# Two of the four weight sums of a seven-product block formed by the loading DMA instead of by VectorE

## The chip, the cores and the metric

The kernel runs on one core of a Trainium2 chip. The metric is device time in microseconds (us) of one launch, from the first to the last instruction of the core. The engines of the core run as separate instruction streams and meet only at semaphores: TensorE (PE, matmuls; PEld, its weight loads), VectorE (DVE), ScalarE (ACT), GpSimd (POOL) and SyncE (SP). Plain loads and stores are issued by SP; GpSimd can issue transfers too, from a queue of its own.

## The reference

The reference is one inference step of a two-layer backbone over 640 tokens (128 context tokens and 512 latent ones) of width 1024. Each layer has an attention mixer followed by a SwiGLU feed-forward part (FFN), and the FFN is where the change lies:

```python
def swiglu(h, w_in, w_out):
    gate, up = jnp.split(h @ w_in, 2, axis=-1)
    return (jax.nn.silu(gate) * up) @ w_out
...
hp = modulate(rms_norm(xp, norm_ffn[l]), sh2_p, sc2_p)
hs = modulate(rms_norm(xs, norm_ffn[l]), sh2_s, sc2_s)
xp = xp + g2_p * swiglu(hp, w_ffn_in[l], w_ffn_out[l])
xs = xs + g2_s * swiglu(hs, w_ffn_in[l], w_ffn_out[l])
```

Everything is float32. `w_ffn_in` is 1024 x 5632 per layer (2816 gate columns and 2816 up columns), `w_ffn_out` is 2816 x 1024.

## The kernel before

**How a matmul is done.** Activations lie transposed, 128 features on the partitions and 640 tokens in the free dimension, in two halves of 320 tokens. Each float32 operand is split into a high part in the fast matmul format (fp32r) and the remainder, and each product is three matmuls (high times high and the two mixed ones). The split of a weight tile is one ScalarE copy (the high part) and one VectorE subtraction (the low part); the helper that does both is `split` (L1361, its two instructions L1367 and L1368).

**The seven-product blocks.** A hidden block `fb` is 128 gate columns and 128 up columns; there are 22 of them per layer. For most of them the products of gate and up weights with the two halves of tokens are not computed as eight quarter products but as seven, by a Strassen-like scheme that needs sums of quarters of the weights and sums of quarters of the activations. With the up weights `u` split into a first half `ua` and a second half `ub`, and the gate weights `g` into `ga` and `gb` (each 128 x 512 in the tile), the function `seven` (L1166) makes four weight sets: wX from `u` as loaded, wW from `gb`, wY from the pair s13 = (`ga` + `gb`, `ua` + `ga`), and wZ from the pair s24 = (`ua` + `ga` + `gb`, that plus `ub`). So four additions of 128 x 512, all on VectorE: L1176 and L1177 for s13, L1180 and L1181 for s24. s13 and s24 are tiles of one tag, "ws", which has two buffers, so that the tile of the next block's s13 is the one that this block's s24 (or s13) has just left.

**Which blocks.** Layer 0 makes blocks 4 to 21 in this way (18), layer 1 blocks 3 to 21 (19); the loop is L1480 to L1509. The output projection of layer 1 uses the same `seven` for 12 more blocks (class `Block`, L1216), four for each of three passes over pairs of hidden blocks. Of these, eight are 1024 columns wide and four 768. That makes 49 uses of `seven`.

**One block of the loop on each engine.** On TensorE a block is seven products of 12 matmuls, in the order p1 (wX), p5 (wY), E of the block before (wW), N (wZ), 21 (wX), 22 (wZ), C (wY). ScalarE and VectorE empty the PSUM banks after each: `p1`, `p5`, `u1` are ScalarE copies, the two additions into `up` and the addition `g2` are VectorE's (L1503, L1505, L1507), the gate function is ScalarE's and its product with `up` is VectorE's (`sg`, L1476). In layer 0 the finished hidden block is split into `hd` (L1427, L1428) and stored in DRAM (`sp`, L1433); in layer 1 seven operands of each pair of blocks are made from it (`op`, L1394, L1395) and stored likewise, to be loaded again in the output projection (`or`, L1278). In layer 0 VectorE also does the modulation sums of a later stage between the blocks (`junk`, L1627, on weights `wm` loaded through the same SP queue).

**What sets the order.** The instructions are emitted in program order and a scheduler places them on the engines; on each engine they then run strictly in the placed order. A tile's buffer is taken again when the last reader of the tile before has finished, which is a semaphore wait of the next writer. If that writer is a DMA, the queue that issues it (SP's or GpSimd's) stands until then, and everything behind it in that queue with it. Weight tiles are split about one block ahead of TensorE.

Of the kernel before, what the change touches and what calls it, by code (L numbers as in the profile page):

```python
# [11 lines left out]
F32 = mybir.dt.float32  # L12
F32R = mybir.dt.float32r
AF = mybir.ActivationFunctionType
ALU = mybir.AluOpType
# [3 lines left out]
P = 128  # L19
# [32 lines left out]
def body(ctx, tc, xT, vecs, crow, wm0, wm0g1, wm0g, wm1, wA, wNV, wNA, wMK, wMV, wOA, wGQ, wGK, wGV, wOC,  # L52
         wFI, wFO, wFO1, cckvT, ckrT, cnkT, cnv, cgkT, cgv, rpbp, tabM, tabK, tabG, maskN,
         yT, o_ckvT, o_krT, o_nkT, o_nv, o_gkT, o_gv):
    nc = tc.nc
    V, S, G = nc.vector, nc.scalar, nc.gpsimd
# [32 lines left out]
    def bank(name, kind="m"):  # L89
        if kind == "m":  # L90
            return psp.tile([P, 512], F32, tag="m", bufs=4, name=name)
        return ypool["pool"].tile([P, 512], F32, tag=kind, bufs=ypool["tags"][kind], name=name)
# [10 lines left out]
    def tmp(name):  # L103
        return tp.tile([P, T], F32, tag="t", bufs=3, name=name)

    def f(ap):
        return ap.bitcast(F32)
# [55 lines left out]
    def load(src, n, name):  # L163
        raw = rawp.tile([P, 1024], F32, tag="raw", name=name)
        nc.sync.dma_start(raw[:, :n], src)
        return raw[:, :n]
# [177 lines left out]
    def mod0(j, bk, load_):  # L344

        box = []

        def part(half):
            def run():
                if half == 0:  # L350
                    box.append(bk())
                psm, rs = box[0], load_(j, half)

                for g in range(4):
                    for b in range(2):
                        o = 512 * (g % 2) + 256 * b
                        rows = slice(64 * b + 32 * (g % 2), 64 * b + 32 * (g % 2) + 32)
                        PE.matmul(psm[rows, :256], scol[:, 4 * half + g, :], rs[g // 2][:, o:o + 256], start=half == 0 and g < 2,
                                  stop=half == 1 and g > 1, tile_position=(0, rows.start))
                if half == 1:  # L360
                    box.append(tp.tile([P, HT], F32, tag="u", bufs=7, name=f"modsb{j}"))
                    S.activation(box[1][:, :256], psm[:, :256], AF.Copy)
            return run

        def end():
            psm, sb = box
            for i in range(2):
                PE.matmul(psm[:, 4 * i:4 * i + 4], sb[:, i * P:(i + 1) * P], sel, start=True, stop=True)
            for i, t in enumerate(MOD0[j]):
                V.tensor_tensor(mods[0][:, t:t + 2, :], psm[:, 0:8].rearrange("p (a i b) -> p a i b", a=2, b=2)[:, :, i, :],  # L370
                                bc2(bmod(0, t, 2)), ALU.add)
        return [part(0), part(1), end]
# [139 lines left out]
    with tc.tile_pool(name="start", bufs=1) as big:  # L512
# [14 lines left out]
        m = [mod0(j, lambda j=j: bank(f"mod{j}", "m"), lambda j, half: [raws[j, half][:, q, :] for q in range(2)]) for j in range(4)]  # L527
# [91 lines left out]
    for kk in range(4):  # L619
# [3 lines left out]
        for j in range(2):  # L623
            k = 2 * kk + j
            a, b = wh[:, 512 * j:512 * (j + 1)], wl[:, 512 * j:512 * (j + 1)]
            for i in range(5):
                c0, c1 = P * i, P * i + P
# [256 lines left out]
    for h in range(8):  # L884
        p, r = divmod(h, 2)
# [116 lines left out]
    for h in range(8):  # L1002
        p, r = divmod(h, 2)
# [159 lines left out]
                w.append(unit(wFI[l, 0, i], 1024, f"wgu{l}_{i}", "vg"[i], pool=fp))  # L1163
        return ph, fk, dr, hd, fs, fp, w, (su, scratch), pre

    def seven(ru, rg, name, fp, split):  # L1166

        n = ru.shape[-1]
        m = n // 2
        wX = split(ru, f"wX{name}")  # L1170
        t = fp.tile([P, 2, 512], F32R, tag="w4", bufs=2, name=f"wW{name}")
        wW = t[:, 0, :m], t[:, 1, :m]
        S.activation(wW[0], rg[:, m:], AF.Copy)
        V.tensor_tensor(wW[1], rg[:, m:], f(wW[0]), ALU.subtract)
        s13 = fp.tile([P, 1024], F32, tag="ws", bufs=2, name=f"s13{name}")[:, :n]
        V.tensor_tensor(s13[:, :m], rg[:, :m], rg[:, m:], ALU.add)  # L1176
        V.tensor_tensor(s13[:, m:], ru[:, :m], rg[:, :m], ALU.add)  # L1177
        wY = split(s13, f"wY{name}")
        s24 = fp.tile([P, 1024], F32, tag="ws", bufs=2, name=f"s24{name}")[:, :n]
        V.tensor_tensor(s24[:, :m], s13[:, m:], rg[:, m:], ALU.add)  # L1180
        V.tensor_tensor(s24[:, m:], s24[:, :m], ru[:, m:], ALU.add)  # L1181
        wZ = split(s24, f"wZ{name}")
        return wX, wW, wY, wZ

    def ffn_out_seven(x, nxt, opened, ops, spilt, split, close, last):
# [6 lines left out]
        def raw(n, c0, m, name):  # L1192
            raws[0] += 1
            t = (rawp.tile([P, 1024], F32, tag="raw", name=name) if raws[0] % 4 else
                 fp.tile([P, 1024], F32, tag="wr", bufs=1, name=name))[:, :m]
            nc.sync.dma_start(t, wFO1[n, :, c0:c0 + m])
            return t
# [18 lines left out]
        class Block:  # L1216


            def __init__(self, i, n, c0):
                self.pairs, self.n, self.name = PASSES[i], n, f"o{i}_{n}"  # L1220
                self.end = i == len(PASSES) - 1
                self.m = m = P * len(self.pairs)
                ru, rg = raw(n, c0, 2 * m, f"ru{self.name}"), raw(n + 4, c0, 2 * m, f"rg{self.name}")
                self.wX, self.wW, self.wY, self.wZ = seven(ru, rg, self.name, fp, split)
                self.held = {}

            def go(self, ps, wt, j, what, first):
# [63 lines left out]
        prev, c0 = None, 0  # L1291
# [41 lines left out]
        for b in ends:  # L1333
# [5 lines left out]
            t = weighed[b.n + 4] = tp.tile([P, HT], F32, tag="u", bufs=7, name=f"xw{b.n}")  # L1339
# [17 lines left out]
    def ffn(l, x, pend, hm, nxt, side, opened):  # L1357
# [123 lines left out]
        for fb in range(few, FB):  # L1481

            ru = load(wFI[l, fb, 1], 1024, f"wu{l}_{fb}r")
            if fb == few or l and fb % 2:
                rg = load(wFI[l, fb, 0], 1024, f"wg{l}_{fb}r")
            else:
                rg = fp.tile([P, 1024], F32, tag="wr", bufs=2 - l, name=f"wg{l}_{fb}r")
                nc.sync.dma_start(rg, wFI[l, fb, 0])
            wX, wW, wY, wZ = seven(ru, rg, f"{l}_{fb}", fp, split)

            g, b5, b2 = bank(f"fg{l}_{fb}"), bank(f"fd{l}_{fb}"), bank(f"fu{l}_{fb}", "y")
            up, sg = tmp(f"up{l}_{fb}"), tmp(f"sg{l}_{fb}")
            p1, p5, u1, g2 = [utile(f"{n}{l}_{fb}") for n in ("p1", "p5", "u1", "g2")]
            product(g, wX, 0, 11, True)
            S.activation(p1, g[:, :HT], AF.Copy)
            product(b5, wY, 0, "D", True)
            S.activation(p5, b5[:, :HT], AF.Copy)  # L1497
            if job:
                close(job)
            product(g, wZ, 0, "N", False)  # L1500
            S.activation(u1, g[:, :HT], AF.Copy)
            product(b2, wX, 512, 21, True)
            V.tensor_tensor(up[:, 0:HT], b2[:, :HT], p1, ALU.add)  # L1503
            product(b5, wZ, 512, 22, False)
            V.tensor_tensor(up[:, HT:T], b5[:, :HT], u1, ALU.add)  # L1505
            product(g, wY, 512, "C", False)
            V.tensor_tensor(g2, g[:, :HT], p5, ALU.add)  # L1507
            S.activation(sg[:, HT:T], g2, AF.Silu, scale=-1.0)
            job = fb, g, wW, up, sg  # L1509
# [48 lines left out]
        pss, ws = {}, {}  # L1558
# [127 lines left out]
    ws = [unit(wGK[v], 1024, f"wgk{v}") for v in range(2)]  # L1686
# [198 lines left out]
    _, before = mod_side([(1, wm1[G2:], G2)], None)  # L1885
# [172 lines left out]
```

## Time and profile before

| What | Value |
|---|---|
| median of 3 runs | 1500.65 us (1499.55 to 1503.75) |
| the profiled execution | 1503.23 us, of which the span of the instructions is 1501.2 us |
| granted TensorE clock | 0.995 of full speed (mean) |
| TensorE busy | 1448.7 us, 96% of the span |
| VectorE busy | 1233.7 us, 82% |
| ScalarE busy | 786.2 us, 52% |
| GpSimd busy | 176.3 us, 12% |
| SP's DMA queue | 225.43 MB, 45.0% of the 16 DMA engines' time |

The FFN loop of layer 0 lies at about 433 to 660 us, that of layer 1 at about 1118 to 1330 us, and the output projection of layer 1 from there to about 1470 us. In a row of a timeline the first number is the start in us, the second the duration, then come engine, line, operation, the tile written and the tiles read, and in brackets how long the engine had been idle and what released it. Names of tiles in the trace are cut: `s` is s13 or s24 of the loop, `s13o` and `s24o` those of the output projection, `wg_12r` and `wu_12r` the loaded gate and up weights of block 12. "SPq" and "POOLq" are DMA issues by SP and GpSimd. In the list of DMA issues the last number is the median time from issue to landing.

### The profile page before, as it was taken

How to read it: one execution, taken by the hardware profiler on the slowest of the kernel's cores; microseconds unless marked ns; L12 is line 12 of the kernel's file. 1: busy time of each engine (PE TensorE's matmuls, PEld its weight loads, DVE VectorE, ACT ScalarE, POOL GpSimd, SP SyncE). 2: the span in 40 equal slices, each digit the busy share in tenths (PEclk: the TensorE clock that was granted, in tenths of full speed). 3: DMA queues.
4: the chain of work that ended last, by engine and by line, in shares of the span. 5: the costliest groups of instructions: out<-in, count | busy, mean ns of one | idle time of the engine just before them, and what ended most of it. 6: DMA issues, size and time to landing. Idle time of an engine off the chain costs nothing. (4 is left out here: it accounts for less than half of the span.)

```text
span 1501.2 us, 25833 instructions
## 1 busy us (share of the span) xinstructions
PE 1448.7 (96%) x9766; PEld 1392.8 (93%) x9766; DVE 1233.7 (82%) x2375; ACT 786.2 (52%) x1539; POOL 176.3 (12%) x272
## 2 busy tenths in 40 slices
PE   5999989899999999999999999999999999999997
PEld 4989978889899999999999999989899999999996
DVE  5877778877788888955898887887899989889976
ACT  5446677763635555532122656673565555655443
POOL 0046636420000000000000122220100000000000
PEclk9999999999999999999999999999999999999999
DMA  9653341015055555549775311115245555548561
GB/s 375 202 152 121 114 145 43 15 64 204 29 207 164 170 171 168 162 169 341 231 229 169 103 33 36 37 41 185 68 157 169 193 170 191 175 154 297 181 263 71
DMA packets 79636, 231.48 MB, mean 154 GB/s; under 512 B 8856, under 2 KB 13240, under 8 KB 79128
## 3 DMA queue, kind: packets, MB, share of 16 engines
q1 hardware_dynamic: 77152, 225.43, 45.0%
q10 hardware_dynamic: 1944, 3.48, 0.7%
q8 instruction: 76, 1.25, 0.3%
q0 software_dynamic: 416, 0.93, 0.2%
q14 instruction: 48, 0.39, 0.1%
HBM read 193.15 MB, written 36.66 MB: 153 GB/s over the span
## 5 line engine op out<-in xcount | busy, mean ns | idle before, releaser
L1627 DVE SCALAR_TENSOR_TENSOR junk<-wm,cb 128x1024 bf16<-128x1024 f32 x88 | 107.2, 1218 | 3.4 <-DMA wm<-in_wm 2.8
L64 PE MATMUL gq<-h10h,wgq 128*128 128x320 f32 x256 | 65.8, 316 | 0.0
L261 POOL TENSOR_SCALAR h10h<-h10t,gs,mods 128x320 fp32r<-128x320 f32 x4 | 3.1, 787 | 437.7 <-DVE h10t L255 435.4
L1367 ACT ACTIVATE wY<-s 128x1024 fp32r<-128x1024 f32 x37 | 39.2, 1060 | 27.7 <-PE fg L64 24.0
L1893 POOL TENSOR_TENSOR xr<-xw,fn1rs 128x320 f32<-128x320 f32 x2 | 1.7, 860 | 416.9 <-ACT fn1rs L229 416.9
L1367 ACT ACTIVATE wZ<-s 128x1024 fp32r<-128x1024 f32 x37 | 39.1, 1057 | 18.6 <-PE fd L64 16.3
L1368 DVE TENSOR_TENSOR wZ<-s,wZ 128x1024 fp32r<-128x1024 f32 x37 | 45.2, 1222 | 2.9 <-ACT wZ L1367 0.2
L1476 DVE TENSOR_TENSOR sg<-up,sg 128x640 f32<-128x640 f32 x37 | 30.4, 822 | 20.8 <-ACT sg L1475 20.3
L64 PEld LDWEIGHTS gq<-h10h,wgq 128*128 128x128 f32 x256 | 44.9, 189 | 0.6
L1368 DVE TENSOR_TENSOR wY<-s,wY 128x1024 fp32r<-128x1024 f32 x37 | 45.1, 1218 | 0.3
L1475 ACT ACTIVATE sg<-fg 128x320 f32<-128x320 f32 x37 | 16.2, 438 | 48.5 <-PE fg L64 48.5
L64 PE MATMUL fg<-h01q,wgu 128*128 128x320 f32 x192 | 40.3, 316 | 0.9 <-ACT h01q L298 0.5
L1497 ACT ACTIVATE p<-fd 128x320 f32<-128x320 f32 x37 | 16.2, 438 | 46.7 <-PE fd L64 46.7
L1830 ACT ACTIVATE gp<-gs,gb,rq 128x640 f32<-128x640 f32 (+1 forms) x40 | 31.8, 795 | 15.3 <-DVE gb L1829 13.6
L64 PE MATMUL gq<-h10l,wgq 128*128 128x320 f32 x128 | 39.5, 308 | 0.0
L64 PE MATMUL fg<-h11q,wX 128*128 128x320 f32 x228 | 36.7, 309 | 0.0
L64 PE MATMUL fu<-h11q,wX 128*128 128x320 f32 x228 | 36.6, 309 | 0.0
L64 PE MATMUL fd<-h11q,wZ 128*128 128x320 f32 x228 | 36.6, 309 | 0.0
L64 PE MATMUL fg<-h11E,wW 128*128 128x320 f32 x228 | 36.5, 309 | 0.0
L64 PE MATMUL fg<-h11N,wZ 128*128 128x320 f32 x228 | 36.5, 309 | 0.0
L64 PE MATMUL fd<-h11D,wY 128*128 128x320 f32 x228 | 36.4, 308 | 0.0
L64 PE MATMUL fg<-h11C,wY 128*128 128x320 f32 x228 | 36.4, 308 | 0.0
(3399 smaller groups left out, 5323.0 us busy)
## 6 DMA issues: line engine op xcount, KB each, us to landing
wm<-in_wm SPq DMA_DIRECT2D x48, 512.0 KB, 4.2
mraw<-in_wm SPq DMA_DIRECT2D x8, 1024.0 KB, 13.1
mraw<-in_wm SPq DMA_DIRECT2D x16, 512.0 KB, 4.1
wmv<-in_wm0g SPq DMA_DIRECT2D x8, 512.0 KB, 3.9
wm<-in_wm0g SPq DMA_DIRECT2D x8, 512.0 KB, 5.3
ruo<-in_wFO SPq DMA_DIRECT2D x8, 512.0 KB, 4.0
rgo<-in_wFO SPq DMA_DIRECT2D x8, 512.0 KB, 6.0
x<-in_xT SPq DMA_DIRECT2D x8, 320.0 KB, 5.2
```

The source lines that it names most:

```text
L64: cls.last = nc.tensor.matmul(*a, **k)
L261: G.tensor_scalar(h[:, c0:c1], t, self.gsl[:, k, 0:1], self.ml[:, self.sh + k, 0:1], ALU.mult, ALU.add)
L1367: S.activation(h, src, AF.Copy)
L1368: V.tensor_tensor(w_, src, f(h), ALU.subtract)
L1475: last = S.activation(sg[:, 0:HT], g[:, :HT], AF.Silu, scale=-1.0)
L1476: V.tensor_tensor(sg, up, sg, ALU.mult)
L1497: S.activation(p5, b5[:, :HT], AF.Copy)
L1627: V.scalar_tensor_tensor(junk, raw, 1.0, cb[:, c, :], ALU.mult, ALU.mult, accum_out=mods[l][:, j0 + i, c:c + 1])
L1830: S.activation(dst, src, AF.Exp, bias=nb, scale=rq[:, j:j + 1], accum_out=ll[:, j:j + 1])
L1893: G.tensor_tensor(x[k][:, c0:c1], root[1][k], nrm.rs[:, c0:c1], ALU.mult)
```

## The change

A new function `first_sums` makes s13. SP loads `gb` into its first half and `ua` into its second half, plainly; then GpSimd issues two transfers that read `ga` from DRAM and add it into the one half and into the other. The two additions on VectorE (L1176, L1177) are gone. Since `ga` is no longer needed by itself, the gate load of a block shrinks to its second half, 128 x 512 (256 KB) instead of 128 x 1024 (512 KB). The up load stays. The s24 additions stay on VectorE and read s13 as before. Per full-width block the DMA engines thus bring 512 + 256 + 4 x 256 = 1792 KB where it was 1024 KB.

```diff
+    def first_sums(name, fp, m, gb, ua, ga):
+
+        t = fp.tile([P, 1024], F32, tag="ws", bufs=2, name=f"s13{name}")[:, :2 * m]
+        nc.sync.dma_start(t[:, :m], gb)
+        nc.sync.dma_start(t[:, m:], ua)
+        for j in range(2):
+            G.dma_start(t[:, j * m:j * m + m], ga, accum_op=ALU.add)
+        return t
+
-    def seven(ru, rg, name, fp, split):
+    def seven(ru, gb, s13, name, fp, split):
 
         n = ru.shape[-1]
         m = n // 2
         wX = split(ru, f"wX{name}")
         t = fp.tile([P, 2, 512], F32R, tag="w4", bufs=2, name=f"wW{name}")
         wW = t[:, 0, :m], t[:, 1, :m]
-        S.activation(wW[0], rg[:, m:], AF.Copy)
-        V.tensor_tensor(wW[1], rg[:, m:], f(wW[0]), ALU.subtract)
-        s13 = fp.tile([P, 1024], F32, tag="ws", bufs=2, name=f"s13{name}")[:, :n]
-        V.tensor_tensor(s13[:, :m], rg[:, :m], rg[:, m:], ALU.add)
-        V.tensor_tensor(s13[:, m:], ru[:, :m], rg[:, :m], ALU.add)
+        S.activation(wW[0], gb, AF.Copy)
+        V.tensor_tensor(wW[1], gb, f(wW[0]), ALU.subtract)
         wY = split(s13, f"wY{name}")
         s24 = fp.tile([P, 1024], F32, tag="ws", bufs=2, name=f"s24{name}")[:, :n]
-        V.tensor_tensor(s24[:, :m], s13[:, m:], rg[:, m:], ALU.add)
+        V.tensor_tensor(s24[:, :m], s13[:, m:], gb, ALU.add)
         V.tensor_tensor(s24[:, m:], s24[:, :m], ru[:, m:], ALU.add)
         wZ = split(s24, f"wZ{name}")
         return wX, wW, wY, wZ
...
-                ru, rg = raw(n, c0, 2 * m, f"ru{self.name}"), raw(n + 4, c0, 2 * m, f"rg{self.name}")
-                self.wX, self.wW, self.wY, self.wZ = seven(ru, rg, self.name, fp, split)
+                ru, gb = raw(n, c0, 2 * m, f"ru{self.name}"), raw(n + 4, c0 + m, m, f"rg{self.name}")
+                s13 = first_sums(self.name, fp, m, wFO1[n + 4, :, c0 + m:c0 + 2 * m], wFO1[n, :, c0:c0 + m], wFO1[n + 4, :, c0:c0 + m])
+                self.wX, self.wW, self.wY, self.wZ = seven(ru, gb, s13, self.name, fp, split)
...
             if fb == few or l and fb % 2:
-                rg = load(wFI[l, fb, 0], 1024, f"wg{l}_{fb}r")
+                gb = load(wFI[l, fb, 0, :, 512:], 512, f"wg{l}_{fb}r")
             else:
-                rg = fp.tile([P, 1024], F32, tag="wr", bufs=2 - l, name=f"wg{l}_{fb}r")
-                nc.sync.dma_start(rg, wFI[l, fb, 0])
-            wX, wW, wY, wZ = seven(ru, rg, f"{l}_{fb}", fp, split)
+                gb = fp.tile([P, 1024], F32, tag="wr", bufs=2 - l, name=f"wg{l}_{fb}r")[:, :512]
+                nc.sync.dma_start(gb, wFI[l, fb, 0, :, 512:])
+            s13 = first_sums(f"{l}_{fb}", fp, 512, wFI[l, fb, 0, :, 512:], wFI[l, fb, 1, :, :512], wFI[l, fb, 0, :, :512])
+            wX, wW, wY, wZ = seven(ru, gb, s13, f"{l}_{fb}", fp, split)
```

The change moves instructions on three queues. The names `s_12_6548` and `s_12_6554` below are s13 and s24 of block 12 before, `s_12_6558` and `s_12_6572` the same two after; lines L1368, L1503, L1505, L1507, L1476, L1428 before are L1375, L1511, L1513, L1515, L1483, L1435 after.

VectorE before, layer 0, from the low part of wZ of block 11 to that of block 12:

```order
L1368 TENSOR_TENSOR wZ_11_6420<-s_11_6417,wZ_11_6420 128x1024 [waits Activation_49]
L1507 TENSOR_TENSOR g_9_6165<-fg_9_6157,p_9_6163 128x320 [waits PE_49]
L1176 TENSOR_TENSOR s_12_6548<-wg_12r 128x512 [waits DMAHW3_49,DVE_49]
L1368 TENSOR_TENSOR wY_11_6414<-s_11_6411,wY_11_6414 128x1024 [waits Activation_49]
L1177 TENSOR_TENSOR s_12_6548<-wu_12r,wg_12r 128x512 [waits DMAHW4_49]
L1180 TENSOR_TENSOR s_12_6554<-s_12_6548,wg_12r 128x512 [waits DVE_49]
L1181 TENSOR_TENSOR s_12_6554<-s_12_6554,wu_12r 128x512 [waits DVE_49]
L1476 TENSOR_TENSOR sg_9_6161<-up_9_6160,sg_9_6161 128x640 [waits Activation_49]
L1174 TENSOR_TENSOR wW_11_6408<-wg_11r,wW_11_6408 128x512 [waits PE_49,Activation_49]
L1428 TENSOR_TENSOR hd_0l<-sg_9_6161,hd_0h 128x640 [waits DMAHW2_49,Activation_49]
L1503 TENSOR_TENSOR up_10_6296<-fu_10_6295,p_10_6298 128x320 [waits PE_49]
L1368 TENSOR_TENSOR wX_12_6542<-wu_12r,wX_12_6542 128x1024 [waits Activation_49]
```

VectorE after, the same place, from there to wZ of block 12:

```order
L1375 TENSOR_TENSOR wZ_11_6436<-s_11_6433,wZ_11_6436 128x1024 [waits Activation_49]
L1515 TENSOR_TENSOR g_9_6177<-fg_9_6169,p_9_6175 128x320 [waits PE_49]
L1375 TENSOR_TENSOR wY_11_6430<-s_11_6419,wY_11_6430 128x1024 [waits DMASW6_49,Activation_49]
L1483 TENSOR_TENSOR sg_9_6173<-up_9_6172,sg_9_6173 128x640 [waits DVE_49,Activation_49]
L1183 TENSOR_TENSOR wW_11_6427<-wg_11r,wW_11_6427 128x512 [waits PE_49,Activation_49]
L1186 TENSOR_TENSOR s_12_6572<-s_12_6558,wg_12r 128x512 [waits DMAHW2_49,DMASW1_49,DVE_49]
L1435 TENSOR_TENSOR hd_0l<-sg_9_6173,hd_0h 128x640 [waits Activation_49]
L1187 TENSOR_TENSOR s_12_6572<-s_12_6572,wu_12r 128x512 [waits DVE_49]
L1511 TENSOR_TENSOR up_10_6310<-fu_10_6309,p_10_6312 128x320 [waits PE_49]
L1375 TENSOR_TENSOR wX_12_6563<-wu_12r,wX_12_6563 128x1024 [waits Activation_49]
L1513 TENSOR_TENSOR up_10_6310<-fd_10_6308,u_10_6314 128x320 [waits PE_49]
L1375 TENSOR_TENSOR wZ_12_6575<-s_12_6572,wZ_12_6575 128x1024 [waits Activation_49]
```

The two additions of s13 are gone, the first addition of s24 has moved behind `sg` and wW of the block before, and it now waits for one of GpSimd's transfers (DMASW).

SP before, layer 0, around the loads of blocks 12 to 14:

```order
L1433 DMA sp_8h<-hd_2h 128x640 [waits DMAHW2_49,Activation_49]
L1488 DMA wg_12r<-in_wFI 128x1024 [waits DVE_49]
L1433 DMA sp_8l<-hd_2l 128x640 [waits DMAHW4_49,DVE_49]
L165 DMA wu_14r<-in_wFI 128x1024 [waits DMAHW5_49,DVE_49]
L1488 DMA wg_13r<-in_wFI 128x1024 [waits DMAHW6_49,DVE_49]
```

SP after, the same place:

```order
L1440 DMA sp_8h<-hd_2h 128x640 [waits DMAHW3_49,Activation_49]
L1440 DMA sp_8l<-hd_2l 128x640 [waits DMAHW4_49,DVE_49]
L165 DMA wu_14r<-in_wFI 128x1024 [waits DMAHW5_49,DVE_49]
L1169 DMA s_12_6558<-in_wFI 128x512 [waits DMASW5_49,DMASW4_49,DVE_49]
L1170 DMA s_12_6558<-in_wFI 128x512 [waits DMAHW7_49]
L1495 DMA wg_13r<-in_wFI 128x512 [waits DMAHW0_49,DVE_49]
```

The two plain loads of s13 stand behind the up load of block 14 and ahead of the gate load of block 13. The VectorE event that the first of them waits for is the low part of wZ of block 11, the last reader of the buffer that s13 of block 12 takes.

GpSimd after, the beginning of layer 0's loop (before, the rows L1172 were not there, and the others stood in this order):

```order
L384 TENSOR_SCALAR mp_3_4103<-mp_3_4103,mr_3r 128x640 [waits DVE_49,PE_49]
L384 TENSOR_SCALAR mpp3p<-mpp3p,mpp3r1r 128x128 [waits DVE_49]
L1172 DMA s_4_5497<-in_wFI 128x512 [waits DMAHW1_49,DMAHW0_49,DMAHW4_49,DMASW0_49,DVE_49]
L1172 DMA s_4_5497<-in_wFI 128x512 [waits DMAHW1_49,DMASW1_49]
L174 TENSOR_TENSOR wgu_1_4736<-wgu_1r,wgu_1_4736 128x1024 [waits DMAHW5_49,PE_49,Activation_49]
L301 TENSOR_SCALAR h01q_4769<-h0132a 128x320 [waits PE_49,Activation_49]
L301 TENSOR_SCALAR h01q_4771<-h0132a 128x320 [waits PE_49,Activation_49]
L301 TENSOR_SCALAR h01q_4773<-h0132a 128x320 [waits PE_49,Activation_49]
L301 TENSOR_SCALAR h01q_4775<-h0132d_4762 128x320 [waits PE_49,Activation_49]
L1172 DMA s_5_5609<-in_wFI 128x512 [waits DMAHW6_49,DMASW2_49,DMAHW7_49,DVE_49,Pool_49]
L1172 DMA s_5_5609<-in_wFI 128x512 [waits DMAHW0_49,DMASW3_49]
```

GpSimd's queue now holds two transfers for each block, each waiting for the plain load of its half; the pair of the first block stands ahead of a weight split (L174) and of four operand sums (L301) that belong to the blocks before the loop.

## The prediction

> **What bounds the kernel now.** I read the page's busy shares first, then the windows over the stages that use the seven-product blocks (stretch, length, busy time of PE, PEld, DVE, ACT and POOL, granted clock, DMA share, GB/s), then the timeline of one block.
>
> ```profile
> PE 1448.7 (96%) x9766; PEld 1392.8 (93%) x9766; DVE 1233.7 (82%) x2375; ACT 786.2 (52%) x1539; POOL 176.3 (12%) x272
> ...
> 460.00:640.00 180.00, 180.00 (x1230) 180.00 (x1230) 161.18 (x233) 94.56 (x147) 0.00 (x0) 1.00 0.52 165
> 1120.00:1300.00 180.00, 180.00 (x1230) 180.00 (x1230) 164.27 (x260) 105.76 (x184) 0.00 (x0) 1.00 0.54 177
> 1300.00:1350.00 50.00, 50.00 (x343) 50.00 (x343) 43.53 (x72) 27.93 (x51) 0.00 (x0) 1.00 0.47 155
> 1350.00:1400.00 50.00, 50.00 (x343) 49.98 (x343) 46.97 (x87) 26.30 (x43) 0.00 (x0) 1.00 0.88 306
> 1400.00:1450.00 50.00, 50.00 (x343) 50.00 (x342) 41.63 (x70) 20.78 (x29) 0.00 (x0) 1.00 0.68 240
> 1450.00:1501.00 51.00, 41.16 (x273) 39.86 (x271) 36.55 (x76) 19.58 (x39) 1.68 (x2) 0.94 0.19 69
> ```
>
> In both FFN loops TensorE is busy in all of the time shown, and the output projection is the same until 1450. VectorE is at 90% there and GpSimd does nothing. So in these stages work taken from VectorE is worth nothing by itself, and the only question is whether something new makes TensorE wait. Idle TensorE is left in the tail (51.0 - 41.2 = 9.8 us).
>
> ```profile
> 523.14 1.92 PE L64 MATMUL fg<-h01q,wX 128*128 128x320 f32 x12
> ...
> 535.45 1.93 PE L64 MATMUL fg<-h01q,wX 128*128 128x320 f32 x12
> ...
> 538.97 1.92 PE L64 MATMUL fg<-h01E,wW 128*128 128x320 f32 x12
> ```
>
> Product p1 comes back after 12.31 us: that is a block on TensorE.
>
> **What is removed.** The chain of one block on VectorE, with the SP issue and the ScalarE copy that matter:
>
> ```profile
> 520.91 1.22 DVE L1368 TENSOR_TENSOR wX<-wu_11r,wX 128x1024 fp32r<-128x1024 f32 x1
> 522.17 0.33 SPq L165 DMA_DIRECT2D wu_14r<-in_wFI  x1
> 522.68 1.23 DVE L1368 TENSOR_TENSOR wZ<-s,wZ 128x1024 fp32r<-128x1024 f32 x1
> 526.25 0.69 DVE L1176 TENSOR_TENSOR s<-wg_12r 128x512 f32<-128x512 f32 x1 [1.95 <-DMA wg_12r<-in_wFI]
> 528.00 0.68 DVE L1177 TENSOR_TENSOR s<-wu_12r,wg_12r 128x512 f32<-128x512 f32 x1
> 528.72 0.69 DVE L1180 TENSOR_TENSOR s<-s,wg_12r 128x512 f32<-128x512 f32 x1
> 529.44 0.69 DVE L1181 TENSOR_TENSOR s<-s,wu_12r 128x512 f32<-128x512 f32 x1
> 530.05 0.82 DVE L1476 TENSOR_TENSOR sg<-up,sg 128x640 f32<-128x640 f32 x1
> 531.68 0.83 DVE L1428 TENSOR_TENSOR hd_0l<-sg,hd_0h 128x640 fp32r<-128x640 f32 x1 [0.20 <-ACT hd_0h L1427]
> 532.42 0.48 DVE L1503 TENSOR_TENSOR up<-fu,p 128x320 f32<-128x320 f32 x1
> 533.22 1.23 DVE L1368 TENSOR_TENSOR wX<-wu_12r,wX 128x1024 fp32r<-128x1024 f32 x1 [0.32 <-ACT wX L1367]
> 534.37 0.48 DVE L1505 TENSOR_TENSOR up<-fd,u 128x320 f32<-128x320 f32 x1
> 534.98 1.23 DVE L1368 TENSOR_TENSOR wZ<-s,wZ 128x1024 fp32r<-128x1024 f32 x1
> 535.65 1.06 ACT L1367 ACTIVATE wY<-s 128x1024 fp32r<-128x1024 f32 x1 [0.70 <-PE fg L64]
> 536.13 0.48 DVE L1507 TENSOR_TENSOR g<-fg,p 128x320 f32<-128x320 f32 x1
> ```
>
> The two additions are 0.69 + 0.68 us of VectorE per block, at most 49 x 1.37 = 67 us in all. All of it lies beside a full TensorE except in the tail; I cost it at nothing. The shorter gate load is one 256 KB transfer less per block, also hidden.
>
> **What is added, and where it stands.** After the change s13 of block 12 is written by transfers, into the buffer that the low part of wZ of block 11 has left (522.68 + 1.23 = 523.91). In the order after, SP's first plain load waits for exactly that event; the two GpSimd transfers wait for the plain loads; the first s24 addition on VectorE waits for the second of the GpSimd transfers; and only when VectorE has then come to the low part of wZ of block 12 can block 13's loads start. That is a ring with one turn per block. Before, the same ring held no transfer: L1176 and L1177 worked from tiles loaded well ahead (one row waited 1.95 us for one).
>
> The VectorE part of a turn, start to start where rows follow each other: first s24 addition 0.72 (528.72 to 529.44), `hd` 0.74 (531.68 to 532.42), second s24 addition 0.61 (529.44 to 530.05), first `up` 0.50, wX 1.15 (533.22 to 534.37), second `up` 0.61 (534.37 to 534.98), wZ 1.23: 5.55 us. The block takes 12.31 us on TensorE, so the ring is hidden as long as the transfers together, from the end of wZ to the landing of the second sum (call it A), take at most 12.31 - 5.55 = 6.8 us. Beyond that every us of A lengthens every block, since `up`, `g` and so TensorE's next E product stand behind the waiting addition. The cushion is small and is spent once: `g` ends at 536.61, E starts at 538.97, so 2.4 us.
>
> **What A is.** No accumulating transfer is in the trace, and the nearest rows are these (KB each, median us from issue to landing):
>
> ```profile
> out_yT<-xr SPq DMA_DIRECT2D x8, 160.0 KB, 2.3
> ...
> wgu_11r<-in_wFI SPq DMA_DIRECT2D x2, 512.0 KB, 3.4
> ...
> wu_12r<-in_wFI SPq DMA_DIRECT2D x2, 512.0 KB, 4.7
> ...
> wg_12r<-in_wFI SPq DMA_DIRECT2D x2, 512.0 KB, 5.5
> ...
> sp_14l<-hd_2l SPq DMA_DIRECT2D x1, 320.0 KB, 6.9
> ...
> sp_18h<-hd_0h SPq DMA_DIRECT2D x1, 320.0 KB, 2.2
> ```
>
> ```profile
> out_o_nv<-nvf POOLq DMA_DIRECT2D x1, 256.0 KB, 6.3
> out_o_nkT<-nkf POOLq DMA_DIRECT2D x4, 64.0 KB, 3.5
> ...
> out_o_gkT<-kn POOLq DMA_DIRECT2D x2, 64.0 KB, 3.7
> out_o_gv<-gvf POOLq DMA_DIRECT2D x1, 128.0 KB, 2.0
> ```
>
> ```profile
> 861.50 0.54 POOL L1740 DMA_DIRECT2D out_o_gkT<-kn  x1 [2.15 <-DVE kn L1738]
> ```
>
> - Wake of SP: wX ended at 522.13 and SP issued the load waiting for its tile at 522.17: 0.05 us. The first plain load's issue then delays the second by some 0.4.
> - Second plain load, 256 KB: 2.2 (shortest row, 320 KB) to 6.9 (longest). From 160 to 512 KB outside the loop the landing grows by 3.4 - 2.3 = 1.1 us, 0.003 us per KB. The loop's 512 KB loads take 4.7 and 5.5; 256 KB less is 0.8 less, so 3.9 to 4.7, and the 512 KB `wu` load issued just before shares the engines; against that the loop's quietest transfers take 2.2. I take 3.5.
> - Wake of GpSimd 0.1 (an estimate, twice SP's). The issue of the first accumulation (0.54) falls while the second half lands.
> - Second accumulation, its issue included: 2.0 to 6.3 by GpSimd's own rows. Those rows are stores and this is a load that also has to read what it adds to. 64 KB takes 3.6 and 192 KB more at 0.003 is 0.6: 4.2, and 0.2 for its twin in front: 4.4.
>
> A = 0.05 + 0.4 + 3.5 + 0.1 + 4.4 = 8.5 us; the ends are 4.75 and 13.75.
>
> Here a page gives another price. The Trainium skill, "DMA: Bandwidth & Descriptors", section on the anatomy of a SWDGE transfer, fits a GpSimd transfer by 2.0 us plus bytes over 436 GB/s. That would be 2.6 us for each of the two, an A of about 5.8, and a ring that is hidden; only the 128 KB row (2.0) is on its side, the 64 KB rows with 3.5 and 3.7 and the 256 KB row with 6.3 are not.
>
> **The sum.**
> - Layer 0, 18 blocks, 17 turns: (8.5 - 6.8) x 17 = 29, less the cushion 2.4: +26.5.
> - Layer 1, 19 blocks, 18 turns. The order there differs: s13 of an odd block takes the buffer that the low part of wY of the even block left, so that two turns hold two A, then s24's first addition and both parts of wY (1.06 + 1.22 = 2.3 after the landing), and in the other turn 0.72 + 1.15 + 0.61 + 0.61 + 1.06 + 1.23 = 5.4. Two blocks are 24.62 us, so A may be (24.62 - 7.7) / 2 = 8.5. At the value taken the nine pairs cost nothing; as transfers scatter and lost TensorE time does not come back, I put +4.
> - Output projection, 12 blocks. The windows show DMA at 0.88 and 306 GB/s in 1350 to 1400, and SP stands in a row of reloads. With A = 0.5 + 6.9 + 0.1 + 6.3 = 13.8 a block would lose up to 7 us; about four blocks lie in the crowded stretch, so 0 to 28. I take +6, near the low end, since the stretches on both sides are less crowded (0.47 and 0.68).
> - Entries. The first block's sums stand ahead of other loads on SP and of one weight split and four operand sums on GpSimd; each entry costs 0 to 5 us by one waiting pair (A less what is ahead), I take +1.5 each: +3.
> - Traffic. 768 KB more per block is 0.79 MB in 12.31 us, 64 GB/s on top of 165; the stretch with 306 shows that this is carried, so it costs nothing beside what the landings hold.
>
> 26.5 + 4 + 6 + 3 = 39.5: 1503.2 + 39.5 = 1542.7 for a profiled execution like this one. That execution lay 2.6 us above the median of the runs, so 1540 us for the median.
>
> **Rivals.**
> 1. *Hidden.* A stays under 6.8: TensorE keeps its 12.31 us, the time stays within 0.3% (4.5 us, about what a measurement of this kernel can tell from no change), 1496 to 1505. For it: the 2.0 and 2.2 us rows, and the page's fit above. Against it: three of the four rows from the loop are above 4, and both steps would have to be quick in every block.
> 2. *Faster, the other side.* The ring is hidden and VectorE's relief shows in the places where TensorE waits for VectorE now. The waits and the tail price it:
>
> ```profile
> PE fg L64 <- DVE g L1507: 0.9, 1, 0.9
> ```
>
> That wait (0.9 us, once) and the four additions in the last 50 us, 4 x 0.68 = 2.7 us, come to some 4 us, at most 5 with the like at the entries: 1495 to 1498. It decides only if A is under 6.8 and the last blocks' transfers are not late either.
> 3. *Heavy.* The accumulation costs much more than a store of its size, as it reads two sources, and the extra 64 GB/s lengthens all landings. At A = 10.5: layer 0 (3.7 x 17) - 2.4 = 60.5, layer 1 (21.0 - 16.9) x 9 = 37, output projection 12, entries 4: +113, 1614 us. For it: the 6.3 us row is GpSimd's only one of 256 KB.
>
> On this the Trainium skill, "Collectives: The Full Stack", in its passage on why ReduceScatter is half of AllGather, says that the addition in the transfer costs no cycles but needs two source reads, and so halves the rate. On 256 KB at 0.003 us per KB that would be 0.8 us more, an A of 9.3 and about 1566 us; no row here can show it.
>
> **How the numbers follow.** Chances: A between 7.1 and 9.7, the forecast with its neighbours, 0.56; heavy 0.22; hidden 0.15; faster 0.07. The forecast's own range is A = 7.1 (1500.7 + 3 + 4 + 3 = 1511) to 9.7 (1500.7 + 47 + 22 + 9 + 3 = 1582). The range for 8 in 10 reaches down into the hidden case, 1499, and up to the heavy case's 1614, taken as 1612. A slowdown over 0.3%: 0.56 + 0.22 = 0.78; within: 0.15; faster: 0.07.
>
> **What would show it.** Right, if in the loop of layer 0 p1 comes back after 13 to 15 us, TensorE's idle time stands before the E product or p5, released by VectorE's `g` or by a weight split, and VectorE's own wait stands before L1186, released by a transfer into s13; if L1169 is issued within 0.1 us of the end of wZ; and if layer 1 loses less per block than layer 0. Wrong, if TensorE is still full in 460 to 640 (hidden), if the wait before L1186 is short and the stall comes from late `wu` or `wg` loads (the queue, not the ring), or if the accumulations land in over 6 us.

## The result and the profile after

The changed kernel takes 1697.28 us (median of 4 runs, 1692.31 to 1705.5) against 1501.68 us: a ratio of 1.131, 95% interval 1.126 to 1.136. It is slower, as forecast, but by 196 us and not by 39; the forecast's range ended at 1612 us. The profiled execution has a span of 1690.5 us against 1501.2, a difference of 189.3.

Where the 189 us lie is seen from a few starts on TensorE. Timeline of the kernel before: first product p1 of layer 0's loop, its last one, the first of layer 1's loop, the first product of the output projection.

```profile
451.02 1.92 PE L64 MATMUL fg<-h01q,wX 128*128 128x320 f32 x12
...
658.58 1.93 PE L64 MATMUL fg<-h01q,wX 128*128 128x320 f32 x12
...
1119.83 1.63 PE L64 MATMUL fg<-h11q,wX 128*128 128x320 f32 x10
...
1351.43 0.60 PE L64 MATMUL fgo<-op9a,wXo 128*128 128x320 f32 x3
```

The same four of the kernel after:

```profile
448.04 1.92 PE L64 MATMUL fg<-h01q,wX 128*128 128x320 f32 x12
...
740.39 1.93 PE L64 MATMUL fg<-h01q,wX 128*128 128x320 f32 x12
...
1201.84 1.63 PE L64 MATMUL fg<-h11q,wX 128*128 128x320 f32 x10
...
1490.52 0.60 PE L64 MATMUL fgo<-op9a,wXo 128*128 128x320 f32 x3
```

| Stretch | before, us | after, us | difference | forecast |
|---|---|---|---|---|
| up to the first p1 of layer 0 | 451.0 | 448.0 | -3.0 | +1.5 |
| 17 turns of layer 0 | 207.6 | 292.4 | +84.8 | +26.5 |
| from there to layer 1's first p1 | 461.3 | 461.5 | +0.2 | +1.5 |
| layer 1 | 231.6 | 288.7 | +57.1 | +4 |
| output projection to the end | 149.8 | 200.0 | +50.2 | +6 |

Waits of the kernel after (engine and line, what was waited for: us in total, times, longest), TensorE's and then VectorE's:

```profile
PE fg L64 <- DVE g L1515: 89.3, 28, 5.7
PE fgo L64 <- DVE p5o L1243: 10.6, 4, 6.3
```

```profile
DVE s L1186 <- DMA s<-in_wFI: 131.5, 25, 8.2
DVE s24o L1186 <- DMA s13o<-in_wFO: 45.7, 10, 7.4
DVE s L1186 <- issue: 39.1, 6, 8.0
```

TensorE waits for `g` and VectorE waits, in the first addition of s24, for the transfers into s13: the places that the forecast named. "issue" in the last row means that the view shows no releaser; by the times of landing in the trace, each of these six waits ended 0.08 us after a second accumulation had landed, so they are the same wait. One turn of layer 0's ring in the timeline of the kernel after:

```profile
573.15 1.22 DVE L1375 TENSOR_TENSOR wZ<-s,wZ 128x1024 fp32r<-128x1024 f32 x1
...
574.40 0.33 SPq L1169 DMA_DIRECT2D s<-in_wFI  x1
...
574.79 0.42 SPq L1170 DMA_DIRECT2D s<-in_wFI  x1
...
578.68 1.76 POOL L1172 DMA_DIRECT2D s<-in_wFI  x2 [15.13 <-DMA s<-in_wFI]
...
586.42 0.69 DVE L1186 TENSOR_TENSOR s<-s,wg_13r 128x512 f32<-128x512 f32 x1 [6.25 <-DMA s<-in_wFI]
...
590.30 1.22 DVE L1375 TENSOR_TENSOR wZ<-s,wZ 128x1024 fp32r<-128x1024 f32 x1
591.43 0.48 DVE L1515 TENSOR_TENSOR g<-fg,p 128x320 f32<-128x320 f32 x1
...
591.97 3.57 PE L64 MATMUL fg<-h01E,wW 128*128 128x320 f32 x12 [4.56 <-DVE g L1515]
```

From the end of wZ (574.37) SP issues after 0.03 us, GpSimd after 4.3, and s24 begins after 12.05: that is A. From there to the end of the next wZ it takes 5.10. A turn is 17.15 us where TensorE needs 12.31. The row of GpSimd holds both issues; the first of the two landed 5.8 us after its issue and the second 7.1 (shortest, median and longest of these two):

```profile
DMA to landing us min/median/max: 5.8/6.4/7.1
```

The windows over layer 0's loop (columns as in the prediction's) and the list of DMA issues say the same in sums:

```profile
460.00:640.00 180.00, 144.21 (x864) 141.58 (x863) 98.15 (x140) 62.42 (x100) 17.59 (x20) 0.89 0.58 159
```

```profile
s<-in_wFI SPq DMA_DIRECT2D x74, 256.0 KB, 3.6
s<-in_wFI POOLq DMA_DIRECT2D x74, 256.0 KB, 6.3
```

TensorE was busy in all of these 180 us and is now in 144.21; the plain loads land in 3.6 us, the accumulations in 6.3, and the DMA engines are little busier than before (0.58 against 0.52), since everything has slowed down together.

### The profile page after: what moved, and what is told of

Same layout as the page of the kernel before. It is cut to its first block, busy times and chain, and to the rows that moved or that the text cites. A ratio compares the mean times of both kernels' runs of the same rounds, so it can differ in the third digit from the quotient of the medians.

```text
span 1690.5 us, 26263 instructions
## 1 busy us (share of the span) xinstructions
PE 1516.2 (90%) x9766; PEld 1446.9 (86%) x9766; DVE 1177.1 (70%) x2277; ACT 773.4 (46%) x1539; POOL 263.5 (16%) x370
## 5 line engine op out<-in xcount | busy, mean ns | idle before, releaser
L1172 POOL DMA_DIRECT2D s<-in_wFI x74 | 65.2, 998 | 645.7 <-DMA s<-in_wFI 379.5
L64 PE MATMUL fg<-h01E,wW 128*128 128x320 f32 x216 | 51.6, 408 | 55.5 <-DVE g L1515 55.5
L64 PEld LDWEIGHTS fg<-h01E,wW 128*128 128x128 f32 x216 | 45.2, 261 | 60.0 <-DVE g L1515 60.0
L64 PE MATMUL fg<-h11E,wW 128*128 128x320 f32 x228 | 47.5, 369 | 33.8 <-DVE g L1515 33.8
L64 PEld LDWEIGHTS fg<-h11E,wW 128*128 128x128 f32 x228 | 42.6, 234 | 36.7 <-DVE g L1515 36.7
L1375 DVE TENSOR_TENSOR wZ<-s,wZ 128x1024 fp32r<-128x1024 f32 x37 | 45.2, 1221 | 16.0 <-ACT wZ L1374 15.9
L1375 DVE TENSOR_TENSOR wY<-s,wY 128x1024 fp32r<-128x1024 f32 x37 | 45.1, 1220 | 8.5 <-ACT wY L1374 7.8
L64 PE MATMUL fg<-h11N,wZ 128*128 128x320 f32 x228 | 44.4, 353 | 6.3 <-ACT p L1503 6.2
L1483 DVE TENSOR_TENSOR sg<-up,sg 128x640 f32<-128x640 f32 x37 | 30.4, 823 | 26.8 <-ACT sg L1482 26.3
L64 PEld LDWEIGHTS fg<-h11N,wZ 128*128 128x128 f32 x228 | 41.6, 227 | 8.0 <-ACT p L1503 8.0
L1172 POOL DMA_DIRECT2D s13o<-in_wFO x24 | 21.1, 1023 | 174.2 <-DMA s13o<-in_wFO 66.5
L64 PE MATMUL fg<-h01N,wZ 128*128 128x320 f32 x216 | 43.7, 363 | 1.6 <-ACT p L1503 1.6
L64 PEld LDWEIGHTS fg<-h01N,wZ 128*128 128x128 f32 x216 | 43.0, 245 | 1.9 <-ACT p L1503 1.9
L1186 DVE TENSOR_TENSOR s24o<-s13o,rgo 128x512 f32<-128x512 f32 (+1 forms) x12 | 7.8, 646 | 45.7 <-DMA s13o<-in_wFO 45.7
```

What stands on the lines that cost most here:

```text
L64: cls.last = nc.tensor.matmul(*a, **k)
L1172: G.dma_start(t[:, j * m:j * m + m], ga, accum_op=ALU.add)
L1186: V.tensor_tensor(s24[:, :m], s13[:, m:], gb, ALU.add)
L1375: V.tensor_tensor(w_, src, f(h), ALU.subtract)
L1483: V.tensor_tensor(sg, up, sg, ALU.mult)
```

## The experiments

The theory: the loss is a ring of one turn per block, through the two shared buffers of s13 and s24. A turn is A plus a fixed VectorE part, and it costs what it exceeds 12.31 us by. The rivals: the added traffic slows all loads (whatever the ring), the accumulation itself is what costs, or VectorE's relief has a worth that is hidden by the rest.

**The accumulations left out.**

```diff
-        for j in range(2):
-            G.dma_start(t[:, j * m:j * m + m], ga, accum_op=ALU.add)
```

> The two accumulating transfers are left out, so that s13 holds gb and ua and not the sums; every wait for a tile stays. Ring theory (the loss is A, the time from the low part of wZ to the landing of s13, less the 6.8 us that the block leaves): A falls to 0.05 + 0.4 + 3.6 = 4.1 us, the ring is hidden, TensorE is full again in both loops and the time is 1495 to 1506 us. Rival, traffic and full queues: two thirds of the added bytes are gone and a third stays (256 of 768 KB a block), so a third of the 196 us stays, about 1565 us.

Measured: 1508.67 us (one run), beside 1499.93 of before: 3 us above the time that the ring theory gave, and far from the rival's 1565. The ring is still there and so are the plain loads, but A is now only their 4 us, and 17 turns of layer 0 take 207.6 us as before:

```profile
460.00:640.00 180.00, 180.00 (x1230) 180.00 (x1229) 148.28 (x206) 93.96 (x147) 0.00 (x0) 1.00 0.57 190
```

TensorE is full again in that stretch. So neither the plain loads nor SP's order cost more than some 9 us in all; the loss needs the accumulations.

**GpSimd's transfers as copies.**

```diff
-            G.dma_start(t[:, j * m:j * m + m], ga, accum_op=ALU.add)
+            G.dma_start(t[:, j * m:j * m + m], ga)
```

> GpSimd issues the same two transfers, into the same halves and with the same waits, but as plain loads that overwrite and do not add (s13 then holds ga twice). If the addition inside the transfer is the price (two reads), the landing falls from 6.3 to about 4.2 us and GpSimd's issue from 0.88 to 0.55; A from 12 to about 9.3, so layer 0 loses some 17 x 2.5 = 43 us in place of 85, and the whole is about 1590 us. If the price is GpSimd's path as such (issue and landing), the time stays within 15 us of 1697.

Measured: 1601.47 us, beside 1499.93, near the first expectation. Half of the loss stays with a mere copy in the ring, half belongs to the addition. Issue by GpSimd (duration in ns, min/median/max) and landing, first of this kernel and then of the changed one:

```profile
L1172 POOL DMA_DIRECT2D s<-in_wFI x74: 536/536/597, 354.1 to 1388.3; - x74
```

```profile
s<-in_wFI POOLq DMA_DIRECT2D x74, 256.0 KB, 4.6
```

```profile
L1172 POOL DMA_DIRECT2D s<-in_wFI x74: 854/888/1234, 353.9 to 1456.8; - x74
```

Adding costs 1.7 us more in landing (6.3 against 4.6). The issue row is 0.35 us longer too (888 against 536 ns), but that does not add up in a turn: the second issue starts 0.59 us after the first with the addition and 0.57 us without it (means over layer 0's loop).

**Half of each accumulation.**

```diff
-            G.dma_start(t[:, j * m:j * m + m], ga, accum_op=ALU.add)
+            G.dma_start(t[:, j * m:j * m + m // 2], ga[:, :m // 2], accum_op=ALU.add)
```

> The changed kernel with each accumulation over half of its columns (128 x 256, 128 KB; the other half of each sum is missing from the result). If the landing of an accumulation goes by bytes above about 2 us, it falls from 6.3 to about 4.2 us, A by some 2.2 us, the time to about 1600 to 1620 us. If it goes by the transfer (a fixed price), the time stays at 1680 or more.

Measured: 1661.63 us, beside 1505.07. Between the two expectations: half the bytes take 36 us off 1697, and the landing falls by 1.2 us only, so most of it does not go by bytes. The time by itself says less than the landing, since most of the gain is layer 0's (26 us) and layer 1, whose order came out differently here, gained 2 (see the second table below).

```profile
s<-in_wFI POOLq DMA_DIRECT2D x74, 128.0 KB, 5.1
```

**One accumulation for both halves.**

```diff
-        for j in range(2):
-            G.dma_start(t[:, j * m:j * m + m], ga, accum_op=ALU.add)
+        two = bass.AP(tensor=ga.tensor, offset=ga.offset, ap=[list(ga.ap)[0], [0, 2], [1, m]])
+        G.dma_start(t.rearrange("p (a b) -> p a b", a=2), two, accum_op=ALU.add)
```

> One accumulating transfer for both halves (its source reads ga twice) in place of two, same bytes. Ring theory with the price per transfer: one issue of 0.88 us and a part of the landing go, A from 12 to about 10.5 to 11; 17 turns of layer 0 and 9 pairs of layer 1 with two A each give 35 x 1.0 to 1.5 us, and the output projection some 10, so about 1635 to 1655 us. If the price is by bytes alone, A stays at 12 and the time within 10 us of 1697.

Measured: 1707.33 us, beside 1499.93: nothing gained. The single issue can go out only when both plain loads have landed, which is when the second of the two went out, and its 512 KB land after 7.8 us instead of 6.3.

**The half that s24 needs, first.**

```diff
-        nc.sync.dma_start(t[:, :m], gb)
         nc.sync.dma_start(t[:, m:], ua)
+        nc.sync.dma_start(t[:, :m], gb)
-        for j in range(2):
+        for j in (1, 0):
```

> As the changed kernel, but the half that s24 needs (ua, then ga added) is loaded and accumulated first. In layer 0 the ring goes through that half alone. If the two accumulations run one behind the other, A loses 0.4 of a plain issue and about 1 us of the second accumulation: 17 x 1.4 = 24 us in layer 0, half as much per block in layer 1 (there every second turn needs both halves), some 6 in the output projection: about 1655 us. If the two share the engines and land together, the gain is under 10 us: 1687 or more.

Measured: 1649.34 us, beside 1502.5. The same transfers in another order are worth 48 us by the median of the changed kernel and 43 by its profiled execution, where 42 were expected: the ring of layer 0 goes through one half. The sum is right in part by luck, as the stages are not as expected: layer 0 gained 35.5 us (292.4 to 256.8) and not 24, layer 1 only 1.8 and not 13.

**One sum by DMA, the other on VectorE.** (Made from the kernel before.)

```diff
         s13 = fp.tile([P, 1024], F32, tag="ws", bufs=2, name=f"s13{name}")[:, :n]
+        nc.sync.dma_start(s13[:, m:], ua)
+        G.dma_start(s13[:, m:], ga, accum_op=ALU.add)
         V.tensor_tensor(s13[:, :m], rg[:, :m], rg[:, m:], ALU.add)
-        V.tensor_tensor(s13[:, m:], ru[:, :m], rg[:, :m], ALU.add)
```

> One part alone: only ua + ga is made by a plain load and one accumulation; ga + gb stays on VectorE, with the full gate load. Ring theory: A holds one plain issue and one accumulation alone: 0.05 + 3.5 + 0.1 + 0.9 + 5 = 9.5 us, so layer 0 loses 17 x 2.7 = 46, layer 1 (9 x 2 = 18), the output projection some 15: about 1575 us. If the loss goes by the number of sums moved (half of 196), 1600; if one accumulation is as bad for the ring as two, above 1650.

Measured: 1645.77 us, beside 1502.5. Taking the other accumulation and its plain load away altogether ends within 4 us of putting them behind. Layer 0 lost 47 us (255.0 for 207.6), as expected, and there it is the time of one chain of two transfers, not a sum over transfers. Layer 1 lost 61.7 us and not 18, more than in the changed kernel. In its trace the waiting s24 addition stands ahead of operand splits there (L1396 after L1181), which the changed kernel's order does not have; what that costs is in the second table below.

These five runs and the changed kernel test the ring by itself. Over the last 15 turns of layer 0 (from about 465 us on), I took from each trace the mean of A (end of wZ to the start of L1186 or its like) and the mean turn:

| Kernel | mean A, us | mean turn, us | turn less A |
|---|---|---|---|
| changed | 12.45 | 17.62 | 5.17 |
| copies | 9.89 | 15.06 | 5.17 |
| half accumulations | 10.98 | 16.16 | 5.18 |
| second sum first | 10.26 | 15.43 | 5.17 |
| one sum by DMA | 10.13 | 15.30 | 5.17 |
| one accumulation | 13.42 | 18.25 | 4.83 |

In all but the last the turn is A + 5.17 to a hundredth, while A varies by 2.5 us (5.10 in 14 of the 15 turns and 6.24 in one). In the last, `hd` stands ahead of the waiting s24 addition and no longer behind it, and the fixed part is 4.48 in 13 of its turns. Nothing else sets the length of a block in that stretch: the traffic matters only through A, and TensorE's clock not at all.

Layer 1's ring, where two blocks hold two A, can be read from the same traces. Means over blocks 10 to 19, five pairs; the fixed part is from the start of the first s24 addition to the end of the low part that frees the buffer, of both blocks together:

| Kernel | A of even blocks, us | A of odd blocks, us | fixed part, us | pair of blocks, us |
|---|---|---|---|---|
| changed | 11.27 | 11.40 | 7.57 | 30.23 |
| copies | 9.71 | 9.97 | 7.60 | 27.28 |
| half accumulations | 9.02 | 10.16 | 11.98 | 31.16 |
| second sum first | 7.91 | 10.29 | 12.41 | 30.60 |
| one sum by DMA | 8.80 | 10.83 | 12.41 | 32.04 |

Here too the pair is the sum of the parts, where TensorE needs 24.62. In the last three the A are shorter, but operand splits have come to stand between the waiting s24 addition and wY, and the fixed part grew by over 4 us: that ate what A had gained. Block 14's first s24 addition and its wY in the changed kernel, then with the second sum first (eleven other instructions stand between):

```profile
1357.50 0.69 DVE L1186 TENSOR_TENSOR s<-s,wg_14r 128x512 f32<-128x512 f32 x1 [1.54 <-DMA s<-in_wFI]
1358.68 1.23 DVE L1375 TENSOR_TENSOR wY<-s,wY 128x1024 fp32r<-128x1024 f32 x1 [0.48 <-ACT wY L1374]
```

```profile
1317.30 0.69 DVE L1186 TENSOR_TENSOR s<-s,wg_14r 128x512 f32<-128x512 f32 x1 [4.27 <-DMA s<-in_wFI]
...
1323.25 1.22 DVE L1375 TENSOR_TENSOR wY<-s,wY 128x1024 fp32r<-128x1024 f32 x1
```

**Buffers of its own for s13.** (The core of the edit; the gate tiles become half as wide, and modulation and layer 1's gate weights go through the raw tiles, to make room.)

```diff
-        t = fp.tile([P, 1024], F32, tag="ws", bufs=2, name=f"s13{name}")[:, :2 * m]
+        t = fp.tile([P, 1024], F32, tag="s3", bufs=2, name=f"s13{name}")[:, :2 * m]
...
-        s24 = fp.tile([P, 1024], F32, tag="ws", bufs=2, name=f"s24{name}")[:, :n]
+        s24 = fp.tile([P, 1024], F32, tag="ws", bufs=1, name=f"s24{name}")[:, :n]
```

> All transfers stay; s13 gets a tag of its own with two buffers and s24 one buffer, so that s13 of a block takes the buffer that was left a block earlier. The room comes from gate tiles of half the width and from loading the modulation weights and, in layer 1, the gate weights through the raw tiles. Ring theory: a turn may now take two blocks, 24.6 us less about 3, far above A = 12; layer 0 is back at 12.31 us a block and the whole at 1497 to 1515 us, the upper end if the shared raw tiles make loads late. Rival, traffic or the accumulations themselves holding the queues: the transfers are the same, so the time stays above 1640 us.

Measured: 1566.97 us, ratio to before 1.044 (95% interval 1.041 to 1.046). Neither expectation holds: 130 of the 196 us go with the ring, 67 do not. In the output projection 9 of the 50 us stay. Two more runs ask what the 67 are.

> The tiles and plain loads of own_buffers, without the two accumulating transfers (s13 then holds gb and ua, not the sums). It tells what the 66 us that own_buffers still loses belong to. If they are the layout's (gate and modulation weights through the three raw tiles), the time stays at 1550 to 1567 us. If they are the accumulations' (their reads and writes beside the other loads, or their landing after two blocks), it falls to 1500 to 1515 us.

Measured: 1496.46 us (one run), beside 1502.5. The layout costs nothing; the 67 us are the accumulations'.

> The tiles of own_buffers, with GpSimd's two transfers as plain loads that do not add (s13 then holds ga twice). Same bytes as own_buffers. If the 66 us that own_buffers loses are the added bytes, the gate loads still land after some 6 us (3.3 without GpSimd's transfers) and the time stays above 1545 us. If they are the addition (twice the engine time per byte), the gate loads land after about 4.5 us and the time is 1498 to 1520 us.

Measured: 1518.91 us, beside 1505.07. So of the 67 us some 48 belong to the addition and the rest to the copy of the same bytes, as the second expectation had it. Windows over 460 to 640 us and one load from the list of issues, first of the kernel with own buffers, then of the same without accumulations:

```profile
460.00:640.00 180.00, 168.08 (x1101) 166.50 (x1099) 125.23 (x176) 80.94 (x128) 21.08 (x24) 0.96 0.69 197
```

```profile
wg_11r<-in_wFI SPq DMA_DIRECT2D x2, 256.0 KB, 6.4
```

```profile
460.00:640.00 180.00, 180.00 (x1230) 180.00 (x1230) 146.64 (x206) 95.00 (x147) 0.00 (x0) 1.00 0.57 188
```

```profile
wg_11r<-in_wFI SPq DMA_DIRECT2D x2, 256.0 KB, 3.3
```

With the ring open, the first addition of s24 waits for the gate load instead, in ten of layer 0's 18 blocks and in 15 of layer 1's 19:

```profile
535.45 0.69 DVE L1186 TENSOR_TENSOR s<-s,wg_12r 128x512 f32<-128x512 f32 x1 [3.43 <-DMA wg_12r<-in_wFI]
```

In four more blocks of layer 0 it still waits for the second accumulation (21.3 us in all). Beside the accumulations a 256 KB gate load takes about twice as long to land, and in layer 0 that load has a ring of its own (its tile is freed by the low part of wW, late in the block). That is the traffic rival, and it is real: by the count of the waits, late gate loads are the larger part of these 67 us and the accumulations' own landing the smaller; the two are not measured apart. In the changed kernel it does not show by itself, since the chain through s13 ends later there.

**The two additions taken out, nothing in their place.**

```diff
-        s13 = fp.tile([P, 1024], F32, tag="ws", bufs=2, name=f"s13{name}")[:, :n]
-        V.tensor_tensor(s13[:, :m], rg[:, :m], rg[:, m:], ALU.add)
-        V.tensor_tensor(s13[:, m:], ru[:, :m], rg[:, :m], ALU.add)
+        s13 = rg
```

> The kernel before without the two additions and with no transfer in their place (s13 is replaced by the loaded gate tile, so the sums are missing from the result). It prices what the change could have gained by taking 66 us of work from VectorE. By the full TensorE of the loops: nothing there and at most 5 us in the tail and at the entries, 1496 to 1501 us. If VectorE was a bound, some 20 us or more less.

Measured: 1504.88 us against 1502.5, ratio 1.002 (95% interval 1.000 to 1.003). Taking 66 us of work from VectorE is worth nothing: layer 1 and the output projection are as long as before to 0.1 us. Layer 0 is 4.5 us longer, which the edit brings about by itself, as wY now reads the gate tile and frees it later (VectorE waits nine times for gate loads there, 16 us in all). The run with own buffers and no accumulations, which lacks the two additions too and keeps the gate tile free, has layer 0 at 207.6 us as before. The best that the change could have done was to make no difference.

No version here beats the kernel before; of those that compute the whole sum, the one with own buffers is the nearest.

## Why the prediction was wrong

**Right: what bounds the kernel, and that the removed work is worth nothing.** TensorE was full, and the two runs without the additions confirm the zero.

**Right: the ring.** The waits are where the prediction put them, SP's issue follows the end of wZ by 0.03 us, and the VectorE part is 5.17 us where 5.55 was worked out from single rows. The limit for A is therefore 12.31 - 5.17 = 7.1 and not 6.8 us.

**Nearly right: the plain loads and the wake of GpSimd.** The sum had 4.05 us from the end of wZ to the issue of the second accumulation; the trace has 4.99 in the mean. The second plain load lands at 4.53 (0.6 us later than put), and GpSimd issues the second accumulation 0.46 us after that, where its wake was put at 0.1.

**Wrong: the size of "second accumulation, its issue included".** This is the step that failed: it was put at 4.4 us, and the trace has 12.45 - 4.99 = 7.46 us, the landing and 0.04 us of wake. That is 3.1 of the 4.0 us that A was short by. Two runs show what is in it (means over layer 0's loop, from issue to landing). An accumulation with no twin in front, in the kernel with one sum by DMA, lands after 5.8 us; the estimate from the 64 KB stores for that was 4.2. With its twin in front it lands after 7.4, so the twin costs 1.6 us; it was put at 0.2. As plain copies the first of a pair lands after 3.8 us and the second after 4.9, so the estimate was nearly right for a transfer that does not add; the addition is worth 2.5 us of the second one. The nearest row was the one I left aside as the upper end, GpSimd's only transfer of 256 KB, 6.3 us; that the accumulations have the same 6.3 as their median is chance, as this median mixes the first and the second of each pair. "The accumulations land in over 6 us" was one of the prediction's own signs of being wrong, and it came true.

**The terms that follow from it.** With A = 12.45 and the measured 5.17 us the prediction's formula gives (12.45 - 7.1) x 17 - 2.4 = 88 us in layer 0, where 84.8 were lost. In layer 1 A is 11.3 in the mean (second table), and the formula gives (22.7 - 16.9) x 9 = 52, where 57.1 were lost. So both formulas hold within a tenth, and it was the term in them that was too small.

**Wrong by itself: the output projection.** I counted four crowded blocks at the low end, 6 us. It lost 50.2 us over 12 blocks, about 4 us each, and VectorE waits there in ten of them (45.7 us, the row above). With own buffers 41 of the 50 us are gone: it is the ring again, in nearly every block, and not the crowd of reloads.

**Wrong in sign, small: the entries.** Nothing was lost there (-3.0 and +0.2 us for +3).

**The rivals.** "Hidden" rested on the 2.0 us row and on the fit of the Trainium skill, "DMA: Bandwidth & Descriptors", section on the anatomy of a SWDGE transfer, 2.6 us for such a transfer. The measurement decides against it for this loop: 4.6 us for a plain GpSimd load of 256 KB and 6.3 for an accumulating one. "Heavy" was the right direction, and the copies show that the addition has a price of its own; that the second read is the reason is not shown by them. Its A of 10.5 and its chance of 0.22 were too low. The extra traffic, which the prediction costed at nothing, shows in the changed kernel only as far as it lengthens A, but by the count of the waits it is the larger part of 67 us in the kernel where the ring is open.

What stays open: why an accumulation of half the size still lands after 5.1 us. The runs show that most of the price does not go by bytes; they don't show what it is. Open too is why the order of layer 1 came out differently in three of the runs.

## What to carry to other kernels

Work moved from an engine to a transfer must be priced by latency where the tile it writes is in a ring: draw the ring, take the engine part from the rows, and compare with the time that the bound engine leaves; here a 1.4 us pair of additions became a chain of 12.45 us. Before that, ask whether the engine relieved is the bound at all; here a run without the work would have told that there was nothing to win. A sum made by an accumulating transfer is two transfers in a row, the plain one and the adding one, so give its tile buffers enough to start a block earlier (130 of the 196 us here), and put the half that is needed first in front (some 45 us here).

## What the hardware showed beside

**An accumulation occupies the DMA engines nearly twice as long as a copy.** GpSimd's queue in the page of the changed kernel and then of the one with copies (packets, MB, share of the 16 engines' span):

```profile
q0 software_dynamic: 14528, 26.11, 9.2%
```

```profile
q0 software_dynamic: 8128, 26.11, 5.3%
```

Other GpSimd transfers take 0.2% in the kernel without accumulations. So 98 accumulations take (9.2 - 0.2)% of 1690.5 us, 152 us, and 98 copies (5.3 - 0.2)% of 1599.7, 82 us: a ratio of 1.9, with more packets for the same bytes. The Trainium skill, "Collectives: The Full Stack", in its passage on why ReduceScatter is half of AllGather, says that an addition in the transfer halves the rate because of its two source reads; the ratio of 1.9 agrees with the halving, for accumulations into a core's own memory, and no run here shows the reads. In landing time it meant 1.7 us, twice what I had worked out from bytes.

**TensorE's clock follows its idle time.** The mean granted clock went from 0.995 to 0.953, and TensorE's busy time from 1448.7 to 1516.2 us for the same matmuls. After an idle of 4.56 us the 12 matmuls of E took 3.57 us (row at 591.97 above) and not 1.92; a block earlier, after an idle of 1.67 us, they took 2.03; after 2.79 us, they and the next product were slow:

```profile
574.83 2.03 PE L64 MATMUL fg<-h01E,wW 128*128 128x320 f32 x12 [1.67 <-DVE g L1515]
```

```profile
626.81 2.38 PE L64 MATMUL fg<-h01E,wW 128*128 128x320 f32 x12 [2.79 <-DVE g L1515]
628.99 3.14 PE L64 MATMUL fg<-h01N,wZ 128*128 128x320 f32 x12
```

So it goes all through layer 0's loop: full speed after the four idles of up to 2.1 us, slow after all 13 of 2.79 us or more. The windows behind the idle of 4.56 us show a granted clock of one half for 5 us, and the full one from 598 us on:

```profile
592.00:597.00 5.00, 5.00 (x19) 5.00 (x20) 4.47 (x7) 2.12 (x6) 1.33 (x2) 0.50 0.58 183
598.00:600.00 2.00, 2.00 (x15) 2.00 (x14) 0.00 (x0) 0.44 (x1) 0.00 (x0) 1.00 0.92 256
```

The Trainium skill, "TensorE: Matmul & The Clock Gate", Part 1 on the HAM clock gate, says that an idle window of about 3.4 us puts the clock back to half until about as long a busy one has passed. This trace agrees on the half, but the step lies between 2.1 and 2.8 us of idle time here, as the trace counts it, and the slow stretch after 591.97 lasted over 5 us. It did not set the time here, as the constant 5.17 us shows, but the busy share of 90% in the page of the profile hides a part of the loss.
